# A two-layer RG-LRU / stick-breaking attention trunk: splits moved between engines, an output projection two tiles at a time, the last attention heads in another order

## The chip, the cores and the metric

The kernel runs on one core of a Trainium2 chip. Time is what the device takes for one execution, in microseconds (us), as the median of several runs. The engines are TensorE (PE; its weight loads are listed apart as PEld), VectorE (DVE), ScalarE (ACT), GpSimd (POOL) and SyncE (SP), which issues most of the transfers. Each engine works through a queue of its own in order; between engines semaphores say what has to be done before.

## What is computed

Two layers on x of 512 positions by 1024 features, all float32. Each layer is a token mixer and a dense FFN, each behind an RMS norm and with its result added to x. The first mixer is a gated linear recurrence, the second stick-breaking attention with 16 heads of 64.

```python
def reference(x, ...):
    for layer in range(DEPTH):
        h = _rmsnorm(x, norm_mix_g[layer])
        ...
        x = x + mix          # layer 0: _rglru_mixer, layer 1: _sb_mixer
        h = _rmsnorm(x, norm_ffn_g[layer])
        x = x + _swiglu(h, ffn_w_gate[layer], ffn_w_up[layer], ffn_w_down[layer])
    return _rmsnorm(x, final_g)

def _rglru_mixer(...):
    gate, xc = gelu(gate_br), conv(x_br)
    a, u = ...                        # from two block matrices w_r, w_i
    hs = _linear_scan(a, u)
    return (hs * gate) @ w_out

def _stick_breaking_attention(q, k, v):   # per block of queries
    z = einsum("bhqd,bhkd->bhqk", qb, k32) * scale
    log_1m = where(mask, log_sigmoid(-z), 0.0)
    suffix = cumsum(log_1m, axis=3, reverse=True) - log_1m
    wts = where(mask, exp(log_sigmoid(z) + suffix), 0.0)
    return einsum("bhqk,bhkd->bhqd", wts, v32)

def _swiglu(h, w_gate, w_up, w_down):     # inner width 2816
    return (silu(h @ w_gate) * (h @ w_up)) @ w_down
```

## The kernel before

**Products in three matmuls.** To hold float32 accuracy every operand is split into a rounded high part and the rest, and a product is wh·xh + wh·xl + wl·xh: mm3, L348 to L351 (the FFN has its own at L762 to L764). Weights come in chunks of 128x1024. For each chunk, split_piece makes wh (a copy on ACT, L303) and wl = raw - wh (L304). Which engine does L304 is set by wl_engine: for chunks 0 to 19 by the table wl_on (L191), in the FFN by Piece.pool, and otherwise by the chunk's parity (odd on POOL) unless wl_dve is set.

**The stream of chunks.** chunk() hands the next split chunk to PE's code, and on the way splits ahead (two chunks, or as many as its argument says) and has SP load ahead. There are three buffers for wh and wl each and four for raw chunks, so a split waits until PE is done with an older chunk.

**Stages.** rglru() comes first: the two branches of w_in, the gates, the scan, the product ah/al of scan and gate (L650 to L653), and the recurrent output projection (from L716): eight tiles m, each one bank of eight k-steps over the pairs ah, al, then an add into x[m]. In this stage the scheduler picks the order by priority. Chunk 18 is a weight tile of the gate branch. Then ffn(0), attention(), ffn(1) and the last norm. In the FFN and in the attention loop the written order stands as it is on PE, ACT, DVE and POOL.

**FFN.** The weights are combined in the manner of Strassen's method. A unit u (six to an FFN, the last one smaller) has pieces for the up and gate products and seven down products; DownPiece q makes the weight d_q of one of these. d5 is the one used just ahead of the product whose bank L922 adds into b (called q2 below: its two halves start at L922). L144 is a subtraction of two raw tiles on POOL that makes the operand of a later piece.

**Attention.** After v, the loop over h (L1252) is written in steps. Step h holds: half of a projection for tile t = h+3 (from h = 13 on, where no projection is left, a part of the output projection instead), s1(h+1) (scores, three banks), chain_a(h+1) (ACT L1138 to L1140, DVE L1141 and L1142, POOL L1143), the projection's other half, s3(h-1) (weights times v, L1201), s2(h) (the suffix sums as matmuls, L1175), chain_b(h) (exponentials on ACT, L1188 and L1189; awl on DVE, L1190), and s3_evac(h-1), which forms o for a head (ACT copy L1214, DVE add L1215). osplit(p) splits o of two heads into oh (ACT L1234) and ol (DVE L1235). out_part(m, lo, hi) multiplies k-steps lo to hi-1 of output tile m; out_evac adds the bank into x[m] (L1248).

**Banks.** Of the eight PSUM banks six hold the scores of two heads (three each, alternating). The last two (list mb) serve projections and s3. From h = 13 on one of them, fill, holds output tile 0, so s3(h-1) must wait until s3_evac(h-2) has emptied the other.

Of the kernel before, what the change touches and what calls it, by code (L numbers as in the profile page):

```python
# [132 lines left out]
class DownPiece(Piece):  # L133
    def __init__(self, unit, q):
        self.unit, self.q, self.c = unit, q, 0
        self.pool = q in (5, 7, 4) and not unit.direct
        self.summed = False
# [33 lines left out]
class Kern:  # L171
    def __init__(self, ctx, tc, a, out):
        self.ctx, self.tc, self.nc, self.a, self.out = ctx, tc, tc.nc, a, out
        mk = lambda name, bufs, **kw: ctx.enter_context(tc.tile_pool(name=name, bufs=bufs, **kw))
        self.const = mk("const", 1)
        self.wp = mk("wp", 1)
        self.tp = mk("tp", 1)
        self.ar = mk("ar", 1)
        self.free = deque((0, i) for i in range(NS1))
        self.free2 = deque()  # L180
        self.clock = 0
        self.keep2 = 0
        self.slot = {}
        pp = mk("pp", 1, space=bass.MemoryType.PSUM)
        self.bank = [pp.tile([P, S], F32, name=f"bank{i}") for i in range(8)]
        self.bi = 0
        self.tn = 0
        self.later, self.done, self.chain = [], set(), {}
        self.wl_dve = False
        self.ring4 = None  # L190
        self.wl_on = {**dict.fromkeys((*range(5, 12), 14), self.nc.gpsimd),  # L191
                      **dict.fromkeys((2, 3, 4, 12, 13, 15, 16, 17, 18, 19), self.nc.vector)}
# [109 lines left out]
    def split_piece(self, i, raw, wh, wl, c):  # L302
        self.nc.scalar.copy(wh[:, c], raw[:, c])  # L303
        self.wl_engine(i).tensor_tensor(wl[:, c], raw[:, c], wh[:, c].bitcast(F32), ALU.subtract)  # L304
# [262 lines left out]
    def rglru(self):  # L567
        nc, tc = self.nc, self.tc
        with ExitStack() as cx:
# [147 lines left out]
            self.bi = 0  # L717
            for m in range(KT):
                p = self.ps()
                self.mm_tile(p, ys)  # L720
                nc.vector.tensor_tensor(self.x[m], self.x[m], p, ALU.add)
                self.ffn_in(m, "g_ffn0")
# [290 lines left out]
    def attention(self):  # L1013
# [5 lines left out]
        with ExitStack() as cx:  # L1019
# [198 lines left out]
            with tc.manual_schedule(engines={E.PE, E.Activation, E.DVE, E.Pool}):  # L1218
# [21 lines left out]
                def out_part(m, lo, hi, bank=None):  # L1240
                    if m not in outs:
                        outs[m] = (bank, *self.chunk(1 if m == 2 else None))
                    pt, wh, wl = outs[m]
                    for k in range(lo, hi):
                        self.mm3(pt, wh[:, ts(k)], wl[:, ts(k)], *ou[k], k == 0, k == KT - 1)

                def out_evac(m):
                    nc.vector.tensor_tensor(self.x[m], self.x[m], outs.pop(m)[0], ALU.add)  # L1248
                    self.ffn_in(m, "g_ffn1")

                nsp = 0
                for h in range(NH + 1):  # L1252
# [6 lines left out]
                    elif h == 13:  # L1259
                        fill = mps()  # L1260
                        out_part(0, 0, 3, fill)
                    elif h == 14:
                        out_part(0, 3, 6)
                    elif h == 15:
                        out_part(1, 0, 6, self.bank[0])
                    elif h == 16:
                        out_part(0, 6, 7)
                        out_part(1, 6, 7)
                        out_part(2, 0, 4, self.bank[1])
                    if h + 1 < NH:  # L1270
                        s1(h + 1)
                        chain_a(h + 1, (0, 1))
                    if t < 16 and h != 1:
# [6 lines left out]
                    if h >= 1:  # L1280
# [6 lines left out]
                    if h < NH:  # L1287
                        s2(h)
                        chain_b(h)
                    if h >= 1:  # L1290
# [3 lines left out]
                    if 6 <= h < 14 and 2 * nsp + 1 < h:  # L1294
                        osplit(nsp)
                        nsp += 1
                    if h == 14:
                        osplit(6)
                out_part(2, 4, 7)
                osplit(7)  # L1300
# [92 lines left out]
```

## Time and profile before

| | |
|---|---|
| time, median of 3 runs | 1119.3 us (1119.23 to 1120.44) |
| the profiled execution's own time | 1120.95 us |
| its span in the profile | 1119.3 us |
| mean granted TensorE clock | 0.997 |
| moved by transfers | 159.87 MB, a mean of 143 GB/s |
| costliest groups outside PE | DVE L304, 118 of wl<-raw,wh: 188.1 us; ACT L303, 144 of wh<-raw: 145.3 us |

A row of the time line reads: start, duration, engine, line, operation, out<-in by the program's names, size, count, and in brackets the idle time of the engine just before with what ended it. Several alike rows are joined into one with a count (x2). A matmul's duration reaches to its modelled end, so the distance of two starts, not the duration, says how fast matmuls follow each other. A row of the table of waits reads: engine and line, what it waited for, total us, times, longest.

### The profile page before, as it was taken

The page shows a single profiled execution, that of the slowest core. Times are in us where ns is not written, and L with a number is a line of the kernel's source. Part 1 is how long each engine was busy: PE and PEld are TensorE (multiplying, and loading weights), DVE is VectorE, ACT ScalarE, POOL GpSimd, SP SyncE. Part 2 cuts the span into 40 slices and gives each one's busy share as a digit, 9 for nine tenths or more (in the row PEclk, how much of TensorE's full clock was granted, in tenths as well). Part 3 has the DMA queues.
Part 4 walks back from the last instruction along what each step waited for, and adds up shares of the span by engine and source line. Part 5 has one row for each costly group of instructions (what it writes and reads, how often), then busy time and mean ns, then how long its engine had stood idle before and what let it go on. Part 6 is the DMA issues. An engine that isn't in the chain of part 4 may idle for free.

```text
span 1119.3 us, 14757 instructions
## 1 busy us (share of the span) xinstructions
PE 1095.9 (98%) x5265; PEld 907.9 (81%) x5265; DVE 907.5 (81%) x1250; ACT 711.7 (64%) x1086; POOL 381.9 (34%) x258
## 2 busy tenths in 40 slices
PE   9999999999999999999999999899999999999996
PEld 6887788878888888888888888778887888888885
DVE  7878886697888888987378898868669787888997
ACT  7598567465646464535389998967764555646454
POOL 2352232335151614205043444312233435261411
PEclk9999999999999999999999999999999999999999
DMA  8522328877676766342243423223986767665421
GB/s 282 171 75 81 126 95 203 192 169 206 157 202 156 201 157 182 83 145 95 79 121 98 118 76 94 77 73 123 212 181 169 192 146 213 157 196 119 150 66 75
DMA packets 48825, 159.87 MB, mean 143 GB/s; under 512 B 6000, under 2 KB 7280, under 8 KB 48752
## 3 DMA queue, kind: packets, MB, share of 16 engines
q1 hardware_dynamic: 36368, 113.84, 29.8%
q0 software_dynamic: 12384, 45.09, 23.1%
q8 instruction: 41, 0.67, 0.2%
q14 instruction: 32, 0.26, 0.1%
HBM read 148.43 MB, written 2.10 MB: 134 GB/s over the span
## 4 chain that ended last, share of the span: by engine, by line
PE 68%; DVE 12%; ACT 4%; issue 4%; DMA 3%; POOL 0%; SPq 0%; DVEq 0%; POOLq 0%; ACTq 0%
PE bank L762 14%; PE bank L763 14%; PE bank L764 14%; PE bank L349 6%; PE bank L351 6%; PE bank L350 5%; DVE wl L304 5%; PE bank L1175 3%; DMA bu<-w_gu 2%; ACT wh L303 2%; PE bank L1201 2%; DVE y L754 1%; PE bank L769 1%; PE bank L1120 1%; DMA bv<-w_gu 1%
## 5 line engine op out<-in xcount | busy, mean ns | idle before, releaser
L304 DVE TENSOR_TENSOR wl<-raw,wh 128x1024 fp32r<-128x1024 f32 (+1 forms) x118 | 188.1, 1599 | 44.1 <-ACT wh L303 43.8
L303 ACT CAST wh<-raw 128x1024 fp32r<-128x1024 f32 (+1 forms) x144 | 145.3, 1012 | 94.5 <-PE bank L764 39.1
L762 PE MATMUL bank<-wh,ow 128*128 128x512 f32 (+1 forms) x480 | 180.0, 375 | 3.4 <-DVE u L754 1.7
L763 PE MATMUL bank<-wl,ow 128*128 128x512 f32 (+1 forms) x480 | 178.6, 372 | 0.6 <-DVE wl L304 0.5
L764 PE MATMUL bank<-wh,ow 128*128 128x512 f32 (+1 forms) x480 | 178.3, 372 | 0.0
L92 POOL DMA_DIRECT2D bu<-w_gu x64 | 55.9, 874 | 271.9 <-DVE wl L304 95.4
L303 ACT CAST wh<-bu 128x1024 fp32r<-128x1024 f32 x66 | 69.4, 1052 | 67.5 <-PE bank L764 37.9
L304 DVE TENSOR_TENSOR wl<-bu,wh 128x1024 fp32r<-128x1024 f32 x66 | 82.0, 1260 | 32.4 <-ACT wh L303 31.5
L762 PEld LDWEIGHTS bank<-wh,ow 128*128 128x128 f32 x480 | 90.4, 188 | 21.2 <-issue 3.2
L349 PE MATMUL bank<-uh,wh 128*128 128x512 f32 x256 | 102.7, 401 | 1.3 <-DVE t L1085 0.6
L763 PEld LDWEIGHTS bank<-wl,ow 128*128 128x128 f32 x480 | 90.4, 188 | 16.5 <-DVE wl L304 1.4
L764 PEld LDWEIGHTS bank<-wh,ow 128*128 128x128 f32 x480 | 90.4, 188 | 15.6
L351 PE MATMUL bank<-uh,wl 128*128 128x512 f32 x256 | 100.2, 392 | 1.0 <-DVE wl L304 1.0
L350 PE MATMUL bank<-ul,wh 128*128 128x512 f32 x256 | 99.8, 390 | 0.3 <-DVE ul L406 0.3
L304 POOL TENSOR_TENSOR wl<-raw,wh 128x1024 fp32r<-128x1024 f32 (+1 forms) x26 | 59.2, 2278 | 111.8 <-ACT wh L303 111.8
L754 DVE TENSOR_TENSOR y<-y,bank 128x512 f32<-128x512 f32 x140 | 88.8, 677 | 2.4 <-PE bank L764 2.3
L762 PE MATMUL bank<-wh,hth 128*128 128x512 f32 x192 | 75.2, 392 | 0.0
L764 PE MATMUL bank<-wh,htl 128*128 128x512 f32 x192 | 74.8, 389 | 0.0
L763 PE MATMUL bank<-wl,hth 128*128 128x512 f32 x192 | 74.7, 389 | 0.0
L304 DVE TENSOR_TENSOR wl<-bv,wh 128x1024 fp32r<-128x1024 f32 x44 | 58.3, 1336 | 15.3 <-ACT wh L303 15.2
L1143 POOL TENSOR_TENSOR spl<-t,sph 128x512 fp32r<-128x512 f32 (+1 forms) x32 | 36.3, 1156 | 85.6 <-DVE sph L1142 79.8
L303 ACT CAST wh<-bv 128x1024 fp32r<-128x1024 f32 x44 | 46.1, 1050 | 20.4 <-DMA bv<-w_gu 9.6
(257 smaller groups left out, 2798.8 us busy)
## 6 DMA issues: line engine op xcount, KB each, us to landing
bu<-w_gu POOLq DMA_DIRECT2D x64, 512.0 KB, 5.8
raw<-w_gu SPq DMA_DIRECT2D x44, 512.0 KB, 3.4
raw<-w_dn SPq DMA_DIRECT2D x24, 512.0 KB, 6.0
bu<-w_gu SPq DMA_DIRECT2D x22, 512.0 KB, 4.2
bv<-w_gu SPq DMA_DIRECT2D x22, 512.0 KB, 4.3
bv<-w_gu POOLq DMA_DIRECT2D x22, 512.0 KB, 6.5
d<-w_dn SPq DMA_DIRECT2D x20, 512.0 KB, 4.0
raw<-w_qk SPq DMA_DIRECT2D x16, 512.0 KB, 3.4
```

The lines of the kernel that those rows point to most:

```text
L92: kern.soon(lambda: kern.nc.gpsimd.dma_start(t, self.part(n), accum_op=ALU.add))
L303: self.nc.scalar.copy(wh[:, c], raw[:, c])
L304: self.wl_engine(i).tensor_tensor(wl[:, c], raw[:, c], wh[:, c].bitcast(F32), ALU.subtract)
L349: mm(out, lhsT=wh, rhs=xh, start=first, stop=False)
L350: mm(out, lhsT=wh, rhs=xl, start=False, stop=False)
L351: mm(out, lhsT=wl, rhs=xh, start=False, stop=last)
L754: add = lambda o, a, b: nc.vector.tensor_tensor(o, a, b, ALU.add)
L762: mm(out, lhsT=xh, rhs=wh, start=first, stop=False, skip_group_check=True)
L763: mm(out, lhsT=xh, rhs=wl, start=False, stop=False, skip_group_check=True)
L764: mm(out, lhsT=xl, rhs=wh, start=False, stop=last, skip_group_check=True)
L1143: nc.gpsimd.tensor_tensor(sl[:, w], sp[:, w], sh[:, w].bitcast(F32), ALU.subtract)
L1175: mm(zt[kt][:, o0:o0 + ZW[j]], lhsT=tri if j == kt else one_n, rhs=s_, start=False, stop=True, skip_group_check=True)
```

## The change

Four things, in four places.

- **Table wl_on:** wl of chunk 18 is made on POOL instead of DVE.
- **Recurrent output projection:** tiles 0 and 1 go together, in two banks: k-steps 0 to 4 of both, then 5 and 6 of both, then 7 of both. Their two adds follow together.
- **FFN:** wl of d5 is made on DVE instead of POOL, in the units that have it there (u = 1 to 4, both FFNs).
- **Attention:** osplit(0) to osplit(5) are put off from the end of a step to the next step, behind chain_a's first two banks; osplit(6) from the end of step 14 to the start of step 15; osplit(7) comes ahead of the last out_parts. Output tile 0 is taken in two sums: its k-steps 0 to 5 close the bank fill and are added to x[0] in step 14; k-steps 6 and 7 go to another bank at the end and are added then. fill then takes tile 1, and tile 2 has bank 0 to itself. s3(14) stands behind s2(15) and chain_b(15). The splits of w_bo[1] and w_bo[2] are written out at the end of steps 13 and 15, with wh on DVE instead of ACT; so on DVE wh and wl of w_bo[2] stand behind the three awl of chain_b(15), where before wl alone stood ahead of them. w_bo[1]'s wl stays on POOL.

```diff
--- before.py
+++ after.py
@@ -133,7 +133,7 @@
 class DownPiece(Piece):
     def __init__(self, unit, q):
         self.unit, self.q, self.c = unit, q, 0
-        self.pool = q in (5, 7, 4) and not unit.direct
+        self.pool = q in (7, 4) and not unit.direct
         self.summed = False
 
     def ready(self):
@@ -186,10 +186,10 @@
         self.bi = 0
         self.tn = 0
         self.later, self.done, self.chain = [], set(), {}
-        self.wl_dve = False
+        self.wl_dve = self.wh_dve = False
         self.ring4 = None
-        self.wl_on = {**dict.fromkeys((*range(5, 12), 14), self.nc.gpsimd),
-                      **dict.fromkeys((2, 3, 4, 12, 13, 15, 16, 17, 18, 19), self.nc.vector)}
+        self.wl_on = {**dict.fromkeys((*range(5, 12), 14, 18), self.nc.gpsimd),
+                      **dict.fromkeys((2, 3, 4, 12, 13, 15, 16, 17, 19), self.nc.vector)}
 
     def ps(self):
         b = self.bank[self.bi % 8]
@@ -300,7 +300,10 @@
         return wh, wl
 
     def split_piece(self, i, raw, wh, wl, c):
-        self.nc.scalar.copy(wh[:, c], raw[:, c])
+        if self.wh_dve:
+            self.nc.vector.tensor_copy(wh[:, c], raw[:, c])
+        else:
+            self.nc.scalar.copy(wh[:, c], raw[:, c])
         self.wl_engine(i).tensor_tensor(wl[:, c], raw[:, c], wh[:, c].bitcast(F32), ALU.subtract)
 
     def split_one(self):
@@ -715,9 +718,17 @@
             self.free_u()
             ys = list(zip(ah, al))
             self.bi = 0
+            two = [(self.ps(), *self.chunk()) for _ in range(2)]
+            for lo, hi in ((0, 5), (5, 7), (7, 8)):
+                for p, wh, wl in two:
+                    for k in range(lo, hi):
+                        self.mm3(p, wh[:, ts(k)], wl[:, ts(k)], *ys[k], k == 0, k == KT - 1)
             for m in range(KT):
-                p = self.ps()
-                self.mm_tile(p, ys)
+                if m < 2:
+                    p = two[m][0]
+                else:
+                    p = self.ps()
+                    self.mm_tile(p, ys)
                 nc.vector.tensor_tensor(self.x[m], self.x[m], p, ALU.add)
                 self.ffn_in(m, "g_ffn0")
             for hl in ys:
@@ -1237,18 +1248,30 @@
 
                 outs = {}
 
-                def out_part(m, lo, hi, bank=None):
+                def out_part(m, lo, hi, bank=None, stop=KT):
                     if m not in outs:
-                        outs[m] = (bank, *self.chunk(1 if m == 2 else None))
-                    pt, wh, wl = outs[m]
+                        outs[m] = [None, *self.chunk(1 if m < 3 else None), 0]
+                    e = outs[m]
+                    if bank is not None:
+                        e[0], e[3] = bank, lo
                     for k in range(lo, hi):
-                        self.mm3(pt, wh[:, ts(k)], wl[:, ts(k)], *ou[k], k == 0, k == KT - 1)
+                        self.mm3(e[0], e[1][:, ts(k)], e[2][:, ts(k)], *ou[k], k == e[3], k == stop - 1)
+
+                def out_add(m):
+                    nc.vector.tensor_tensor(self.x[m], self.x[m], outs[m][0], ALU.add)
 
                 def out_evac(m):
-                    nc.vector.tensor_tensor(self.x[m], self.x[m], outs.pop(m)[0], ALU.add)
+                    out_add(m)
+                    outs.pop(m)
                     self.ffn_in(m, "g_ffn1")
 
+                def out_split():
+                    self.wh_dve = True
+                    self.split_one()
+                    self.wh_dve = False
+
                 nsp = 0
+                due = None
                 for h in range(NH + 1):
                     t = h + 3
                     if t < 16:
@@ -1258,18 +1281,22 @@
                             proj_evac1(t)
                     elif h == 13:
                         fill = mps()
-                        out_part(0, 0, 3, fill)
+                        out_part(0, 0, 3, fill, 6)
                     elif h == 14:
-                        out_part(0, 3, 6)
+                        out_part(0, 3, 6, None, 6)
                     elif h == 15:
-                        out_part(1, 0, 6, self.bank[0])
+                        osplit(6)
+                        out_part(1, 0, 6, fill)
                     elif h == 16:
-                        out_part(0, 6, 7)
-                        out_part(1, 6, 7)
-                        out_part(2, 0, 4, self.bank[1])
+                        out_part(2, 0, 4, self.bank[0])
                     if h + 1 < NH:
                         s1(h + 1)
+                        if h == 14:
+                            out_add(0)
                         chain_a(h + 1, (0, 1))
+                    if due is not None:
+                        osplit(due)
+                        due = None
                     if t < 16 and h != 1:
                         proj(t, 1)
                         proj_evac1(t)
@@ -1277,7 +1304,7 @@
                         chain_a(h + 1, (2,))
                     if h >= 13:
                         mb[:] = [b_ for b_ in (self.bank[6], self.bank[7]) if b_ is not fill]
-                    if h >= 1:
+                    if 1 <= h and h != 15:
                         s3(h - 1)
                     if t < 16 and t % 2:
                         proj_evac2(t)
@@ -1287,17 +1314,21 @@
                     if h < NH:
                         s2(h)
                         chain_b(h)
+                    if h == 15:
+                        s3(h - 1)
+                    if h in (13, 15):
+                        out_split()
                     if h >= 1:
                         s3_evac(h - 1)
                     if t < 16 and t % 2 == 0:
                         proj_evac2(t)
                     if 6 <= h < 14 and 2 * nsp + 1 < h:
-                        osplit(nsp)
+                        due = nsp
                         nsp += 1
-                    if h == 14:
-                        osplit(6)
+                osplit(7)
                 out_part(2, 4, 7)
-                osplit(7)
+                out_part(1, 6, 7)
+                out_part(0, 6, 7, self.bank[1])
             for m in range(3):
                 out_part(m, 7, 8)
                 if m == 0:
```

The order of DVE at the end of the recurrent block, from the last gate product but one to the first add into x. al_489, al_529 and al_613 are the low parts for k = 5, 6 and 7, the chunk's wl belongs to w_ao. Before:

```order
L651 TENSOR_TENSOR bank_75<-bank_75,sv_852 128x512
L701 TENSOR_TENSOR bank_76<-bank_76,acc 128x512
L304 TENSOR_TENSOR wl_1137<-raw_1028,wh_1136 128x1024
L653 TENSOR_TENSOR al_489<-bank_74,ah_488 128x512
L653 TENSOR_TENSOR al_529<-bank_75,ah_528 128x512
L651 TENSOR_TENSOR bank_76<-bank_76,sv_871 128x512
L653 TENSOR_TENSOR al_613<-bank_76,ah_612 128x512
L721 TENSOR_TENSOR x_78<-x_78,bank_70 128x512
```

In the changed kernel:

```order
L654 TENSOR_TENSOR bank_75<-bank_75,sv_852 128x512
L656 TENSOR_TENSOR al_489<-bank_74,ah_488 128x512
L656 TENSOR_TENSOR al_529<-bank_75,ah_528 128x512
L704 TENSOR_TENSOR bank_76<-bank_76,acc 128x512
L307 TENSOR_TENSOR wl_1101<-raw_1028,wh_1100 128x1024
L654 TENSOR_TENSOR bank_76<-bank_76,sv_871 128x512
L656 TENSOR_TENSOR al_613<-bank_76,ah_612 128x512
L732 TENSOR_TENSOR x_78<-x_78,bank_70 128x512
L732 TENSOR_TENSOR x_79<-x_79,bank_71 128x512
```

al of k = 5 and 6 now stand ahead of the gate add (L701, now L704) and of the wl; the two adds into x follow each other.

The order of DVE in the FFN, unit 1 of the first FFN, from the wl that follows the sum into b to q2 (L922). d_190 is d5's source, its wl is wl_2090. Before:

```order
L304 TENSOR_TENSOR wl_2069<-raw_1755,wh_2068 128x1024
L754 TENSOR_TENSOR y_1499<-y_1499,bank_76 128x512
L754 TENSOR_TENSOR y_1500<-y_1500,bank_77 128x512
L304 TENSOR_TENSOR wl_2109<-raw_1944,wh_2108 128x1024
L304 TENSOR_TENSOR wl_2129<-raw_1980,wh_2128 128x1024
L922 SCALAR_TENSOR_TENSOR b_1497<-b_1497,nrs,bank_72 128x512
L922 SCALAR_TENSOR_TENSOR b_1498<-b_1498,nrs,bank_73 128x512
```

In the changed kernel (all lines 3 to 11 higher):

```order
L307 TENSOR_TENSOR wl_2069<-raw_1755,wh_2068 128x1024
L765 TENSOR_TENSOR y_1499<-y_1499,bank_76 128x512
L765 TENSOR_TENSOR y_1500<-y_1500,bank_77 128x512
L307 TENSOR_TENSOR wl_2090<-d_190_1751,wh_2089 128x1024
L307 TENSOR_TENSOR wl_2109<-raw_1944,wh_2108 128x1024
L307 TENSOR_TENSOR wl_2129<-raw_1980,wh_2128 128x1024
L933 SCALAR_TENSOR_TENSOR b_1497<-b_1497,nrs,bank_72 128x512
L933 SCALAR_TENSOR_TENSOR b_1498<-b_1498,nrs,bank_73 128x512
```

One wl, d5's, has come in ahead of the two that stand before q2; on POOL the same row is gone.

The order of ACT in step 13 of the attention, from the copy for o(11) (t_6425) to the first exponential of chain_b(13) (awh). oh is osplit(5), wh_6432 a chunk of w_bo, t are chain_a(14)'s. Before:

```order
L1214 COPY t_6425<-bank_76 64x512
L1234 CAST oh_6428<-o_6246 128x512
L303 CAST wh_6432<-raw_6039 128x1024
L1138 ACTIVATE t_6459<-bank_70 128x512
L1139 ACTIVATE t_6459<-t_6459 128x512
L1140 ACTIVATE t_6459<-t_6459 128x512
L1138 ACTIVATE t_6469<-bank_71 128x384
L1139 ACTIVATE t_6469<-t_6469 128x384
L1140 ACTIVATE t_6469<-t_6469 128x384
L1138 ACTIVATE t_6479<-bank_72 128x384
L1139 ACTIVATE t_6479<-t_6479 128x384
L1140 ACTIVATE t_6479<-t_6479 128x384
```

In the changed kernel:

```order
L1225 COPY t_6425<-bank_76 64x512
L1149 ACTIVATE t_6449<-bank_70 128x512
L1150 ACTIVATE t_6449<-t_6449 128x512
L1151 ACTIVATE t_6449<-t_6449 128x512
L1149 ACTIVATE t_6459<-bank_71 128x384
L1150 ACTIVATE t_6459<-t_6459 128x384
L1151 ACTIVATE t_6459<-t_6459 128x384
L1245 CAST oh_6469<-o_6246 128x512
L1149 ACTIVATE t_6473<-bank_72 128x384
L1150 ACTIVATE t_6473<-t_6473 128x384
L1151 ACTIVATE t_6473<-t_6473 128x384
L1199 ACTIVATE awh_6507<-bank_73 128x512
```

The oh copy has moved from ahead of the chain to behind its first two banks, and the chunk's copy is gone from ACT at this place.

## The prediction

> **What bounds the kernel now.** I read the page's first part, then the table of what TensorE (PE) waits for, then the time line of PE at those waits.
>
> ```profile
> span 1119.3 us, 14757 instructions
> PE 1095.9 (98%) x5265; PEld 907.9 (81%) x5265; DVE 907.5 (81%) x1250; ACT 711.7 (64%) x1086; POOL 381.9 (34%) x258
> PE bank L1120 <- DVE awl L1190: 2.9, 3, 2.3
> PE bank L762 <- DVE b L922: 1.7, 3, 1.0
> 698.07 0.39 PE L349 MATMUL bank<-uh,wh 128*128 128x512 f32 x1
> 698.30 0.39 PE L350 MATMUL bank<-ul,wh 128*128 128x512 f32 x1
> ```
>
> PE is busy 98% and sets the end; the change takes no matmul away, so only PE's waits can be won. They are small and scattered (waits rows: total, times, longest). Undisturbed 128x512 matmuls start 0.23 us apart (698.07, 698.30), exactly 0.227 over longer stretches; what two starts are further apart than that I call lost. The change touches three of the places: the recurrent block, the FFN's L922, and attention's last heads. All else on PE I take as it is.
>
> **Recurrent block: wl of chunk 18 to POOL, output projection two tiles at a time.**
>
> ```profile
> 103.56 1.99 ACT L303 CAST wh<-raw 128x1024 fp32r<-128x1024 f32 x2
> 108.95 0.39 PE L350 MATMUL bank<-ul,wh 128*128 128x512 f32 x1
> 109.09 2.33 DVE L304 TENSOR_TENSOR wl<-raw,wh 128x1024 fp32r<-128x1024 f32 x2
> 110.34 0.50 PE L351 MATMUL bank<-uh,wl 128*128 128x512 f32 x1 [1.00 <-DVE wl L304]
> 116.61 2.39 POOL L304 TENSOR_TENSOR wl<-raw,wh 128x1024 fp32r<-128x1024 f32 x1 [20.59 <-ACT wh L303]
> 116.73 3.36 DVE L304 TENSOR_TENSOR wl<-raw,wh 128x1024 fp32r<-128x1024 f32 x1
> 124.59 0.50 PE L349 MATMUL bank<-ah,wh 128*128 128x512 f32 x1
> 125.47 1.28 DVE L653 TENSOR_TENSOR al<-bank,ah 128x512 fp32r<-128x512 f32 x2
> 126.21 0.50 PE L350 MATMUL bank<-al,wh 128*128 128x512 f32 x1 [1.12 <-DVE al L653]
> 128.01 0.69 DVE L653 TENSOR_TENSOR al<-bank,ah 128x512 fp32r<-128x512 f32 x1 [0.65 <-ACT ah L652]
> ```
>
> PE could have run the first matmul on chunk 18's wl at 108.95+0.23=109.18 and ran it at 110.34: 1.16 lost, 0.16 more than the bracket, because a restarted matmul takes longer (0.50 against 0.39); after such a restart the next start is another 0.11 late. wl stood last in a DVE queue. POOL idles 20.59 before 116.61, so it can take wl as soon as its wh is there: the first of the two casts of 103.56 ends near 104.6, and with 2.39 to 3.5 (the free and the held length, next paragraph) wl is done by 107.0 to 108.1, before 109.18. That wait goes: 1.27.
>
> What is late next: while a POOL op with SBUF operands runs, a DVE op whose two inputs lie in SBUF stands still, and the reverse. Row 116.73 shows it: one wl takes 3.36, against 2.33/2=1.17 each at 109.09, beside POOL's 2.39 at 116.61. So DVE may lose up to 2.39 there, wins the 1.17 of the moved wl, and is some 1.2 late. The projection then starts at 120.9-1.27=119.6 (124.59, less its wait of 0.29, less 15 matmuls of 0.227, gives 120.9). Before, it lost at 124.59 (0.29), at 126.21 (126.21-124.59-0.23=1.39, and 0.11 behind), and 0.43 at the last ah: 2.22. With two tiles interleaved, 30 matmuls (6.8 us) stand ahead of the first use of k=5 instead of 15: needed at 119.6+6.8+0.2=126.6 (al of k=5), 127.3 (k=6) and 119.6+42x0.227=129.2, al 129.4 (k=7). DVE delivered these at 126.1, 126.75 (row 125.47) and 128.70 (row 128.01). Delivered at the same times they cost nothing; all 1.2 late they cost about 0.7. But the order shows al of k=5 and 6 moved ahead of a gate add (0.6) and a wl split (1.2), which pays for the 1.2, so I take nothing. Sum 1.27+2.22=3.5; between 1.5 (both lost in part) and 4: **-3.5**.
>
> **FFN: wl of d5 from POOL to DVE, in 8 units (u=1 to 4 of both FFNs).**
>
> ```profile
> 242.78 1.05 ACT L303 CAST wh<-d 128x1024 fp32r<-128x1024 f32 x1
> 245.94 2.73 POOL L304 TENSOR_TENSOR wl<-d,wh 128x1024 fp32r<-128x1024 f32 x1
> 246.60 6.50 DVE L304 TENSOR_TENSOR wl<-raw,wh 128x1024 fp32r<-128x1024 f32 x2 [1.26 <-ACT wh L303]
> 248.75 3.27 POOL L144 TENSOR_TENSOR d<-raw,raw 128x1024 f32<-128x1024 f32 x1
> 253.03 1.39 DVE L922 SCALAR_TENSOR_TENSOR b<-b,nrs,bank 128x512 f32<-128x512 f32 x2
> 253.91 0.47 PE L762 MATMUL bank<-wh,ow 128*128 128x512 f32 x1 [0.32 <-DVE b L922]
> 856.77 7.20 DVE L304 TENSOR_TENSOR wl<-raw,wh 128x1024 fp32r<-128x1024 f32 x2 [1.42 <-ACT wh L303]
> 864.77 0.47 PE L762 MATMUL bank<-wh,ow 128*128 128x512 f32 x1 [1.01 <-DVE b L922]
> 983.20 0.47 PE L762 MATMUL bank<-wh,ow 128*128 128x512 f32 x1 [0.36 <-DVE b L922]
> ```
>
> L922 (named q2 here) is queued on DVE behind two wl, which take 6.50 and 7.20 instead of 2.33: POOL's wl (2.73) and L144 (3.27) hold them. In three units PE waits for q2: 0.32+1.01+0.36, and 0.16 more at each, 2.2 in all. In the new order d5's wl stands on DVE just ahead of those two. Its wh is there at 243.83, and DVE idles 1.26 before 246.60, so its 1.17 fits into idle time. POOL is left with L144, which can hold DVE for 3.27 at most: 2.33+3.27=5.6 at most against 6.50, with d5's wl paid from the idle slot, so q2 comes 0.9 to 2.6 earlier, more than two of the waits and, at 856.77 (7.20), more than the third. L144's result feeds pieces that come later than q2. Value **-2.2**; the upper end is the second rival's.
>
> **Attention, steps 12 to 16.**
>
> ```profile
> 697.30 0.47 PE L349 MATMUL bank<-uh,wh 128*128 128x512 f32 x1 [0.61 <-DVE t L1085]
> 710.61 0.50 PE L1120 MATMUL bank<-qh,ks 128*128 128x512 f32 x1 [0.19 <-DVE awl L1190]
> 711.27 0.28 DVE L1154 CAST r<-t 128x256 fp32r<-128x256 f32 x1
> 713.10 0.62 ACT L1234 CAST oh<-o 128x512 fp32r<-128x512 f32 x1 [1.78 <-DVE o L1215]
> 713.12 0.85 PE L1201 MATMUL bank<-awh,vs 128*128 128x512 f32 x4 [0.17 <-DVE o L1215]
> 713.63 1.04 ACT L303 CAST wh<-raw 128x1024 fp32r<-128x1024 f32 x1
> 718.68 0.39 PE L351 MATMUL bank<-oh,wl 128*128 128x512 f32 x1
> 719.51 0.58 ACT L1188 ACTIVATE awh<-bank 128x512 fp32r<-128x512 f32 x1
> 721.37 0.50 PE L1120 MATMUL bank<-qh,ks 128*128 128x512 f32 x1 [2.30 <-DVE awl L1190]
> 726.75 0.46 PE L1175 MATMUL bank<-sph,tri 128*128 128x512 f32 x1
> 729.94 0.50 PE L349 MATMUL bank<-oh,wh 128*128 128x512 f32 x1 [0.68 <-DVE awl L1190]
> 734.03 1.23 DVE L304 TENSOR_TENSOR wl<-raw,wh 128x1024 fp32r<-128x1024 f32 x1 [0.26 <-ACT wh L303]
> 723.40:726.80 3.40, 3.40 (x15) 3.11 (x15) 2.60 (x6) 3.25 (x7) 0.68 (x1) 0.54 0.01 2
> ```
>
> Lost now: at 697.30, 0.8; around 710.61 and 713.12, 1.5 with the bank waits inside s1; from 718.91 (the end of 718.68's pitch) to 726.75, 7.84 go for an s1 and an s3 that take 1.63 and 1.22 where nothing disturbs them, so 5.0, of which 1.6 is the granted clock of 0.54 (last row: time, then busy us of PE, PEld, DVE, ACT, POOL, then the clock); at 729.94, 0.95. Together 8.25.
>
> The cause is ACT's order: at the end of step 12 ACT waits 1.78 for o, does oh, then copies wh for 1.04, and only then starts the chain of the next head; so chain_b(13) reaches 719.51, DVE's awl follows, and s1(15) waits 2.30. In the new order osplit stands behind the first two chains and the wh copy of w_bo[1] is on DVE. ACT's chain_b(13) comes earlier by 1.78+1.04 and by about 1.1 gained ahead of it: 715.6. Worked through the new order, PE waits: at 697.30 none; step 13 0.8; step 14: s1(15) needs three banks, and their awl come at 717.4, 718.7 and 719.4 (715.6 with the same 1.8 behind it as from 719.51 to 721.3, and two more); PE is there at 717.4 (718.91 less the 1.5 won before), 718.0 and 719.1, so it waits 0.75 and 0.25, then 1.0 for s3(13), because DVE does the wh copy (0.6) and o(12) (0.7) behind that last awl, to 721.0, where PE is ready at 720.05; step 15 none; step 16 2.3, because w_bo[2]'s wh and wl now both stand on DVE behind awl(15) (near 733.4): wh +0.6, wl +1.23, so 734.0 and 735.2, where PE is ready near 732.4. Sum 5.1, so 8.25-5.1: **-3.1**.
>
> A wh copy of 128x1024 on DVE has no row. A CAST of 128x256 takes 0.28 (711.27), so four times its elements at most 1.1; a two-input op of 128x1024 takes 1.23; the same cast starts its next op 0.20 later, so it may be as short as 0.5. I take 0.6; at 1.2 each of the two copies costs 0.6 more. The two k=6 parts at the end and the second x[0] add (one 0.7 DVE op under matmuls) cost nothing as long as PE has out_part(2) to run.
>
> **Behind the recurrent block.** The first FFN starts under a chain of transfers.
>
> ```profile
> 170.92 5.80 DMA bu<-w_gu
> 213.95 5.52 DMA bu<-w_gu
> ```
>
> Between 222 and 232 PE waits some 2 us for what these bring. The first is issued by POOL behind an op that follows PE's sums, so it should move with PE; where it doesn't, up to 3.5 is given back. I take **+0.5**.
>
> Sum: -3.5-2.2-3.1+0.5=-8.3. The profiled execution took 1120.95 for a span of 1119.3; by -8.3 it becomes 1112.65, a span of 1111.0. The median of the runs is 1119.3, 1.65 below the profiled execution's own time, so the forecast for the median is **1111.0**.
>
> **Rivals.**
> 1. The recurrent gain is swallowed by the transfers of the first FFN. For it: PE waits there although it stands far behind in the queue. Against it: the issue hangs on PE's own progress. +3: 1114.
> 2. Slower: d5's wl makes DVE later. If POOL's ops (L144, then the next wl) still hold both wl, the added 1.2 and up to 0.7 of a longer hold (3.27 against 2.73) put q2 1.2 to 1.9 late in all 8 units. The three without slack pay in full, the others in part (no PE wait there now): at 1.9 some 3x1.9+5x1.0=11 over before's level in place of -2.2, so 1119.3-6.1+11=1124. It turns the sign from about 1.2 per unit (3x1.2+5x0.5=6.1). Against it: DVE's idle slot of 1.26 and one POOL op fewer. The Trainium skill (page "SBUF — State Buffer", section "Who interferes with whom") says that a VectorE instruction with two SBUF inputs and a GpSimd one that reads SBUF exclude each other, the first to issue holding the port to its end; that speaks against moving work to DVE wherever POOL still runs, and the 6.50 of row 246.60 agrees. By the rule with L144 first, it is the loss of the gain, 1113; by L144 behind d5's wl, 1111.
> 3. The new waits of step 14 (2.0 within 4 us) or step 16 (2.3) bring the clock down again, as the 2.30 at 721.37 did: 1.6 each, or the copy is 1.2. 1113 to 1114.5. The Trainium skill (page "TensorE: Matmul & The Clock Gate", section "HAM oscillation — how this bites in real kernels") sets the danger at idle gaps above about 3.4 us; by that none of these waits would throttle and the sum stays. The trace differs: clock 0.54 behind a wait of 2.30, so I keep the rival.
> 4. The change doesn't do what it says: the scheduler in the recurrent block already fills PE's waits with the next tile's matmuls, and the new waits of steps 14 and 16 eat the attention term: 1116.
>
> **Numbers.** Forecast 1111 (within 1.5): 0.52; clock or copy: 0.18; transfers: 0.14; the fourth, or two together (1116): 0.07; d5 slower: 0.05; better, with steps 13 to 16 free of waits (1106): 0.04. The range 1107.5 to 1116.5 leaves out 1124, 1106 and some of the rest, less than 0.2. A measurement of this kernel tells apart about 0.2% (2.2 us): faster means under 1117.1. That is all but 2 and part of 4: 0.89; within 0.06; slower 0.05.
>
> **What would show it.** Right: PE has no wait for wl near 109 and none for al near 126; the row "PE bank L762 <- DVE b" is gone, and the two wl ahead of q2 take about 5; no clock under 0.9 near 723; PE waits about 2 us for w_bo[2]'s wl near the end of attention. Wrong, if wl of d5 takes over 3 us on DVE; if PE's wait between 222 and 232 grows by what was won at 110 and 126; if the granted clock drops in step 14 or 16; if the wh copy on DVE takes over 1.

## The result, and the profile after

The changed kernel takes 1113.25 us in the median (1110.91 to 1116.54, 6 runs), the kernel before 1120.22 in the runs beside it (1119.23 to 1121.40, 6 runs): a ratio of 0.994, 95% interval 0.9924 to 0.9957. That is 7.0 us less; forecast were 8.3 less and 1111.0. The profiled execution took 1113.21 for a span of 1111.5, 7.8 less than the span before.

The first rows are the engines' busy time and the waits of PE in the changed kernel (engine, line, what it waited for: total us, times, longest). Line 762 of before is 773 now, 349 is 352, 350 is 353, 351 is 354, 1120 is 1131.

```profile
PE 1092.8 (98%) x5265; PEld 908.7 (82%) x5265; DVE 901.6 (81%) x1260; ACT 710.0 (64%) x1084; POOL 359.9 (32%) x251
PE bank L354 <- DVE wl L307: 2.0, 3, 1.1
PE bank L352 <- DVE wh L304: 1.4, 1, 1.4
PE bank L1212 <- DVE o L1226: 0.8, 2, 0.7
PE bank L1131 <- DVE awl L1201: 0.4, 1, 0.4
```

The rows of L762 for L922 and of L350 for al are gone, and s1's waits for awl have gone from 2.9 to 0.4. New are a wait for wh made by DVE and, in place of the one for wl at 110, two at 121 and 731 (the third lies in the first 10 us). The next rows, from time lines of PE and DVE in the changed kernel, place them: the recurrent block, the two wl ahead of q2, and attention's step 16.

```profile
121.30 0.50 PE L354 MATMUL bank<-ah,wl 128*128 128x512 f32 x1 [1.07 <-DVE wl L307]
241.41 1.22 DVE L307 TENSOR_TENSOR wl<-d,wh 128x1024 fp32r<-128x1024 f32 x1
242.80 4.52 DVE L307 TENSOR_TENSOR wl<-raw,wh 128x1024 fp32r<-128x1024 f32 x2 [0.17 <-ACT wh L306]
717.00 0.85 PE L1212 MATMUL bank<-awh,vs 128*128 128x512 f32 x4 [0.65 <-DVE o L1226]
729.96 0.50 PE L352 MATMUL bank<-oh,wh 128*128 128x512 f32 x1 [1.44 <-DVE wh L304]
731.22 0.51 PE L354 MATMUL bank<-oh,wl 128*128 128x512 f32 x1 [0.53 <-DVE wl L307]
```

To see where the 7.8 come from, take the start of one and the same matmul in both profiles (each has 5265) at the borders of five stretches. The table gives the change of each stretch against the kernel before, for every profile of this study; times in the head are those of the kernel before, and "rest" is the start of the span, where the clock starts up at another moment each time (-0.4 to 2.8 up to 104 us), and up to 0.4 between 330 and 680.

| profile | 104 to 132: recurrent block | 215 to 247: start of the first FFN | 247 to 330 and 840 to 990: units with d5 | 680 to 752: attention's end | rest | span |
|---|---|---|---|---|---|---|
| before (us) | 27.8 | 31.9 | 233.1 | 72.1 | | 1119.3 |
| changed | -2.2 | -1.6 | -2.5 | -1.8 | +0.3 | 1111.5 |
| changed, again | -2.3 | -2.0 | -2.4 | -3.4 | +1.0 | 1110.3 |
| recurrent part alone | -2.2 | -2.2 | -0.1 | -0.5 | +0.6 | 1114.9 |
| wl of chunk 18 alone | +3.0 | -0.9 | -1.2 | +1.1 | +0.3 | 1121.6 |
| two tiles alone | -2.2 | -2.1 | +0.7 | +1.2 | +3.1 | 1119.8 |
| d5 alone | 0.0 | -0.2 | -2.1 | -0.1 | -0.2 | 1116.7 |
| attention alone | 0.0 | -0.8 | 0.0 | -3.3 | 0.0 | 1115.2 |
| changed, d7 too | -2.2 | -0.7 | -1.9 | -1.8 | +0.7 | 1113.4 |
| changed, wh copies on ACT | -2.3 | -2.0 | -2.5 | -2.5 | +1.3 | 1111.4 |
| changed, osplit at the end of its step | -2.2 | -2.3 | -2.5 | +0.9 | +0.3 | 1113.5 |
| changed, w_bo[2] split early | -2.2 | -0.4 | -2.5 | -5.8 | +1.8 | 1110.3 |
| three mends | -3.6 | -2.4 | -1.4 | -6.4 | +0.3 | 1105.8 |

A stretch that a kernel leaves as it was still differs from the kernel before: the units with d5 by -1.2 to +0.7, attention's end by -0.5 to +1.2 (there the clock was low for one cell of 3.41 us or for two). A single entry of about 1 therefore shows nothing by itself; the waits behind it have to say the same.

### The profile page after: what moved, and what is told of

The parts are those of the page before. It is cut to its first block, busy times and chain, and to the rows that moved or that the text cites. A ratio compares the mean times of both kernels' runs of the same rounds, so it can differ in the third digit from the quotient of the medians.

```text
span 1111.5 us, 14758 instructions
## 1 busy us (share of the span) xinstructions
PE 1092.8 (98%) x5265; PEld 908.7 (82%) x5265; DVE 901.6 (81%) x1260; ACT 710.0 (64%) x1084; POOL 359.9 (32%) x251
## 4 chain that ended last, share of the span: by engine, by line
PE 76%; DVE 9%; ACT 3%; issue 2%; DMA 1%; POOL 0%; DVEq 0%; ACTq 0%; POOLq 0%
PE bank L773 16%; PE bank L774 16%; PE bank L775 16%; PE bank L352 7%; PE bank L354 7%; PE bank L353 7%; DVE wl L307 4%; PE bank L1186 3%; PE bank L1212 2%; DVE y L765 1%; PE bank L780 1%; DMA bu<-w_gu 1%; PE bank L1131 1%; ACT wh L306 1%; PE bank L1132 1%
## 5 line engine op out<-in xcount | busy, mean ns | idle before, releaser
L307 DVE TENSOR_TENSOR wl<-raw,wh 128x1024 fp32r<-128x1024 f32 (+1 forms) x117 | 176.4, 1511 | 37.6 <-ACT wh L306 37.4
L307 POOL TENSOR_TENSOR wl<-raw,wh 128x1024 fp32r<-128x1024 f32 (+1 forms) x27 | 62.1, 2301 | 101.9 <-ACT wh L306 99.4
L765 DVE TENSOR_TENSOR y<-y,bank 128x512 f32<-128x512 f32 x140 | 88.9, 679 | 2.4 <-PE bank L775 2.3
L1154 POOL TENSOR_TENSOR spl<-t,sph 128x512 fp32r<-128x512 f32 (+1 forms) x32 | 39.1, 1244 | 84.1 <-DVE sph L1153 81.2
```

Source lines behind the costliest of these rows:

```text
L765: add = lambda o, a, b: nc.vector.tensor_tensor(o, a, b, ALU.add)
L1154: nc.gpsimd.tensor_tensor(sl[:, w], sp[:, w], sh[:, w].bitcast(F32), ALU.subtract)
```

## The experiments

**The parts alone.** Three kernels take the kernel before and add one part each.

Recurrent part:

```diff
-        (5..11, 14) POOL; (..., 16, 17, 18, 19) DVE
+        (5..11, 14, 18) POOL; (..., 16, 17, 19) DVE
+            two = [(self.ps(), *self.chunk()) for _ in range(2)]
...
```

> The kernel before with the recurrent block's part alone (wl of chunk 18 on POOL, two tiles at a time). Theory (the parts add up, each where the profile after shows it): the wait of 1.00 at 110.34 goes, those at 124 to 128 go, one of about 1.1 comes on the first wl of w_ao, so 2.1 us are won up to 130; and the 2.1 lost between 222 and 232 falls to about 0.6, since the transfers move with PE. Span 1119.3-3.6=1115.7, ratio about 0.997. Rival (the gain near 222 came from another part, or by chance): the loss between 222 and 232 stays at 2.1 or grows, span 1117.2 or more, ratio 0.998 to 1.0.

Measured: 1117.28, ratio 0.9975 (0.9963 to 0.9987), span 1114.9. The waits in the block are those seen in the changed kernel, to 0.1 us: -2.2. The stretch from 215 on gains 2.2 too; whether that belongs to the change is taken up below.

d5:

```diff
-        self.pool = q in (5, 7, 4) and not unit.direct
+        self.pool = q in (7, 4) and not unit.direct
```

> The kernel before with d5's wl on DVE alone. Theory: the three waits for L922 go (2.2 us), the two wl ahead of it take 4 to 5 us instead of 6.5; span 1117.1, ratio 0.998. Rival (DVE only gets later, and the waits went because the units start at another time in the changed kernel): the waits stay or grow, ratio 1.0 or more.

Measured: 1118.5, ratio 0.9988 (0.9975 to 1.0000), span 1116.7. The interval reaches 1, so the times alone don't show the gain; the trace does. The row of L762 for L922 is gone from PE's waits. One new wait of 0.92 for another DVE op (L754, at 241.82) stands ahead of d5's place, behind a transfer that took 6.79 (226.16 to 232.95); the units from 247 on gain 2.1.

Attention (all that the change does from out_part on, and no more):

```diff
-                        osplit(nsp)
+                        due = nsp
...
+                    if h in (13, 15):
+                        out_split()
```

> The kernel before with the attention part alone. Theory: the waits from step 12 to 14 fall from 8.2 to about 2.8, and step 16 brings a wait of 1.4 and one of 0.5 for w_bo[2]'s split on DVE, with the clock near 0.5 for some 3.4 us behind them (1.6 us); net -1.5 to -2, span 1117.5, ratio 0.998. Rival (the half-speed stretch behind step 16 is an accident of one execution): no clock under 0.9 there, net -3.3, span 1116, ratio 0.997.

Measured: 1117.15, ratio 0.9973 (0.9961 to 0.9984), span 1115.2, attention -3.3. Both waits of step 16 are there (1.44 and 0.53) but the clock stays up behind them, so the rival was right. The granted clock is the last figure but two of each row: first the changed kernel's profile, then this one, each with the waits in the first two rows.

```profile
728.40:731.80 3.40, 1.43 (x7) 0.79 (x5) 3.09 (x5) 0.90 (x2) 0.00 (x0) 1.00 0.02 5
731.80:735.20 3.40, 3.40 (x10) 2.62 (x8) 0.00 (x0) 0.00 (x0) 0.00 (x0) 0.50 0.43 154
```

```profile
729.80:733.20 3.40, 2.80 (x21) 2.56 (x19) 1.81 (x4) 3.05 (x7) 0.00 (x0) 1.00 0.00 0
733.20:736.60 3.40, 2.03 (x8) 1.38 (x9) 2.60 (x4) 0.20 (x1) 0.00 (x0) 1.00 0.11 17
```

The clock's records change on a grid of 3.41 us. In the changed kernel both waits fell into one cell of it (of the 7 matmuls in the row 4 begin there, the others are left over from the cell before), and the next cell ran at 0.50. Here the border at 733.2 cuts the first wait (732.60 to 734.04), and the second lies in the next cell.

By their ratios the three parts save 0.25, 0.12 and 0.27%, 0.64% together, and the whole change 0.60%: they add up within the intervals. The spans of the single profiles add up to more (11.1 against 7.8), because the start of the first FFN (3.2 in the three together, 1.6 in the whole) and attention's end with its clock (3.9 and 1.8) come out otherwise in each execution.

**The recurrent block taken apart.** One kernel only moves the wl of chunk 18, the other only takes the two tiles together.

```diff
-        (5..11, 14) POOL; (..., 16, 17, 18, 19) DVE
+        (5..11, 14, 18) POOL; (..., 16, 17, 19) DVE
```

> The kernel before with wl of chunk 18 on POOL and nothing else. Theory (POOL's op wins the wait at 110 and holds two of DVE's two-input ops up by 2.2, so that what follows on DVE is late): the 1.27 at 110 goes; the first wl of w_ao comes late and costs about 1.3 there, and the waits for al near 124 to 128 stay at 2.2 or are hidden by it in part; 104 to 131.5 gains 0 to 1.3 in all. Rival (the wait on w_ao's wl comes from the two-tile order): no such wait, 1.3 won.

Measured: one run, 1123.31 (before 1119.20 to 1123.42 beside it); the block is 3.0 longer, so theory and rival both missed. The wait at 110 goes (-1.3), but at the other end the kernel loses more than before:

```profile
105.53 3.42 DVE L642 TENSOR_TENSOR xc<-xc,sv 128x512 f32<-128x512 f32 x2
118.22 2.84 DVE L304 TENSOR_TENSOR wl<-raw,wh 128x1024 fp32r<-128x1024 f32 x1
121.11 0.50 PE L351 MATMUL bank<-ah,wl 128*128 128x512 f32 x1 [1.03 <-DVE wl L304]
128.56 0.51 PE L349 MATMUL bank<-ah,wh 128*128 128x512 f32 x1 [2.12 <-ACT ah L652]
130.50:133.90 3.40, 3.40 (x9) 2.68 (x9) 2.57 (x3) 2.07 (x5) 2.38 (x1) 0.50 0.01 2
```

Two adds of xc take 3.42 where 1.27 is usual (row 105.66 of before), held by POOL's wl, which runs from 104.55 to 107.80. DVE is 2.2 late behind them and still some 1 late once the wl that it no longer makes is taken off. The first wl of w_ao ends at 121.06 in place of 120.09, and PE waits 1.03 for it and 2.12 for the last ah, with no second tile to cover it. The low clock behind these waits is about 1.6 of the loss (an estimate: 8 of the 9 matmuls in the last row begin in that cell, where 15 fit at 0.227).

```diff
-                p = self.ps()
-                self.mm_tile(p, ys)
+            two = [(self.ps(), *self.chunk()) for _ in range(2)]
...
```

> The kernel before with the first two tiles of the recurrent output projection together, wl of chunk 18 still on DVE. Theory: the wait of 1.00 at 110.34 stays, w_ao's first wl comes in time, the three waits at 124 to 128 go: 2.2 won between 118 and 131.5. Rival: the wait on w_ao's wl is there too, 0.9 won.

Measured: one run, 1121.5 (1119.8 span, with a start-up 2.8 longer than before's). The block gains 2.2 with the wait at 110 still there and no wait for w_ao's wl. So the two tiles alone bring what the whole part brings: the move of wl to POOL wins 1.3 at 110 and gives 1.3 back at 121. The theory was right.

**d7 to DVE too.**

```diff
-        self.pool = q in (7, 4) and not unit.direct
+        self.pool = q == 4 and not unit.direct
```

> The changed kernel with d7's wl on DVE too (POOL then keeps d4's alone). It asks how far the FFN's gain carries. Theory (d5 won because DVE had an idle slot of 1.26 at its place and POOL's op held two of DVE's): at d7's place the sequence on DVE gets 1.2 longer; where it has an idle slot nothing is lost, so within 1 us of the changed kernel, ratio to before 0.993 to 0.995. Rival (each op moved to DVE wins, since POOL holds DVE up for longer than the op costs it): 1 to 3 us faster, 0.991 to 0.993. The second rival of the prediction, at this place: new waits of PE for DVE in 8 units, 3 us or more slower, 0.997 or more.

Measured: 1112.79, ratio 0.9921 (0.9902 to 0.9940). No wait for L933 (q2) comes; the units with d5 are 0.6 slower than in the changed kernel, most of it one wait (0.31) for L765 ahead of d5's place. The ratio lies in the range of the first rival (0.991 to 0.993), but its interval overlaps that of the changed kernel, and the trace shows nothing won at d7's place, as the theory had it. The slower rival is out at this place too.

**Attention's last steps.** First w_bo[2] is split at the start of step 15, where ACT idles 1.53 (row 724.59 of the changed kernel) ahead of oh.

```diff
                         osplit(6)
+                        self.split_one()      # ahead of osplit(6)
...
-                    if h in (13, 15):
+                    if h == 13:
```

> The changed kernel, with w_bo[2] split at the start of step 15 instead of its end: wh on ACT, in its idle 1.5 us ahead of oh, wl on DVE ahead of ol. Theory (the split's late place makes the wait in step 16, and the wait makes the low clock): both waits of step 16 go (1.6+0.7 with their restarts) and the clock stays at 1.0 (1.6 and 0.2 more), so 4.1 us under the changed kernel: span 1107.4, ratio to before 0.989. Rival (DVE is the limit there wherever the split stands): awl of step 15 come 1.2 later and the wait only moves to s3(15) or stays for awl, span 1109.5 to 1111.5, ratio 0.991 to 0.994.

Measured: 1110.37, ratio 0.9906 (0.9892 to 0.9921), span 1110.3 with a start 1.6 later than the changed kernel's. Attention's end gains 4.0 over the first profile of the changed kernel and 2.4 over the second; both waits are gone, and none takes their place.

Then two kernels put back one half of the new order each: the wh copies on ACT again, and osplit(0) to osplit(5) at the end of their steps.

```diff
-                    self.wh_dve = True      # in out_split: wh on ACT again
...
-                        due = nsp           # the other kernel
+                        osplit(nsp)
```

> The changed kernel with the wh copies of w_bo[1] and w_bo[2] back on ACT, at the same places (end of steps 13 and 15). Theory (it is the order on ACT that won; a copy of 1.05 there puts the next head's chain 1.05 later, which the 0.60 on DVE doesn't): s3(13) starts up to 0.3 earlier, but chain_a(15) and with it what s2(15) needs 1.05 later; w_bo[2]'s wl ends about 0.4 later on the path awl(15), wh, wl. Steps 12 to 16 lose 0.5 to 1.5 against the changed kernel, the low clock aside. Rival (the engine of the copies doesn't matter): the same within 0.2.

Measured: one run, 1113.09. Attention's end is at -2.5, with low clock behind step 16:

```profile
717.30 0.85 PE L1212 MATMUL bank<-awh,vs 128*128 128x512 f32 x4 [0.34 <-DVE o L1226]
730.48 0.75 PE L352 MATMUL bank<-oh,wh 128*128 128x512 f32 x1 [1.64 <-ACT wh L306]
```

The profile of the changed kernel that has the low clock too is at -1.8, so this one is 0.7 better, where the theory had it 0.5 to 1.5 worse and the rival the same within 0.2. s3(13) waits 0.34 in place of 0.65, as the theory said; but the late chain_a(15) is covered, and for w_bo[2] PE waits 1.64 once in place of 1.44 and 0.53. One profile each: that the copies on DVE cost 0.7 is not shown, but they won nothing here.

> The changed kernel with osplit(0) to osplit(5) back at the end of their steps; the rest as changed. Theory (ACT's idle wait for o ahead of oh, 1.78 at the end of step 12, was the larger half): the 0.8 at 697 comes back and chain_b(13) is about 2.4 late, so that s1(15) waits some 2.5 to 3 in place of 1.0; steps 11 to 14 lose 2.5 to 3.5 against the changed kernel. Rival (the wh copies were the cause): under 1 lost.

Measured: one run, 1115.18. Attention's end is at +0.9, 2.7 worse than the first profile of the changed kernel and 4.3 worse than the second. The waits of before are back, though s1(15) waits 1.33 and not 2.30 as before, nor the 2.5 to 3 of the theory:

```profile
692.46 0.47 PE L352 MATMUL bank<-uh,wh 128*128 128x512 f32 x1 [0.59 <-DVE t L1096]
715.58 0.50 PE L1131 MATMUL bank<-qh,ks 128*128 128x512 f32 x1 [1.33 <-DVE awl L1201]
719.20:722.60 3.40, 3.40 (x12) 3.00 (x12) 3.08 (x7) 2.57 (x6) 3.39 (x3) 0.50 0.21 57
```

So the deferred osplit is the part that won; the clock falls here behind step 14, and stays up behind step 16. That s1(15) waits 1.0 less than before fits the copy of 1.04 that ACT no longer makes (not tested by itself).

**The changed kernel again.**

> The changed kernel once more, for what differs between executions. Theory: the waits at 121, 714, 717 and the two of step 16 are the same within 0.1; the stretch from 215 to 235 differs by up to 1.5 from the first profile, since the same stretch differs as much among kernels that are alike up to there; the clock falls behind step 16 only if both waits lie in one stretch of the clock's grid. Rival: 215 to 235 repeats within 0.2, and the low clock comes each time.

Measured: one run, 1111.98. The waits at 121, 714 and 717 repeat within 0.1, and this time the clock stays up, with the same two waits of step 16:

```profile
727.00:730.40 3.40, 1.96 (x16) 1.72 (x14) 2.43 (x5) 2.73 (x7) 0.00 (x0) 1.00 0.00 0
730.40:733.80 3.40, 2.88 (x11) 2.09 (x12) 1.79 (x2) 0.00 (x0) 0.00 (x0) 1.00 0.34 92
```

215 to 247 differs by 0.4 from the first profile, less than the theory allowed.

**Three mends together:** w_bo[2] split early, w_bo[1]'s split behind o(12) instead of ahead of it, and the wl of w_ao's first tile on POOL, of its second on DVE.

```diff
-        (5..11, 14, 18) POOL; (..., 16, 17, 19) DVE
+        (5..11, 14, 18, 20) POOL; (..., 16, 17, 19, 21) DVE
...
+                        self.split_one()      # step 15, ahead of osplit(6)
...
                         s3_evac(h - 1)
+                    if h == 13:
+                        out_split()
```

> The changed kernel with three mends: w_bo[2] split at the start of step 15 as in the run before; w_bo[1]'s split behind o(12) instead of ahead of it; and the wl of the first two w_ao tiles exchanged (the first on POOL, the second on DVE). Theory: 4.1 in step 16 with the low clock, 0.6 of the 0.85 that s3(13) waits for o(12), and the 1.35 for w_ao's first wl: 6 under the changed kernel, span 1105.5 when the first FFN starts as in the profile of the changed kernel; ratio to before 0.9875. Rival (the wait for w_ao's wl only moves to al, which has 0.3 to 1 us to spare): 1.3 less won, ratio 0.989.

Measured: 1108.32 (1107.38 to 1109.21), ratio 0.988 (0.9861 to 0.9900), span 1105.8: the fastest kernel of the study, 0.6% under the changed one by the two ratios, whose intervals don't meet. The recurrent block comes to -3.6, so the rival is out. The whole kernel's longest waits for DVE, the start-up aside, are now among these:

```profile
PE bank L773 <- DVE u L765: 1.8, 2, 0.9
PE bank L773 <- DVE b L765: 0.7, 1, 0.7
PE bank L1131 <- DVE awl L1201: 0.4, 1, 0.4
PE bank L1212 <- DVE o L1226: 0.2, 1, 0.2
```

## Why the prediction was right, point by point

- **What bounds, and the sign.** PE's busy share is 98% still. Of the 7.8, 4.7 are idle time of PE and 3.1 busy time, in which restarts after a wait count; no matmul went. Right.
- **Recurrent block, -3.5 forecast, -2.2 measured.** The waits at 110 and at 124 to 128 went as said. The term was mis-sized in "what is late next". That DVE comes some 1.2 late was about right: two adds lose 2.2 beside POOL (3.44), the wl that DVE no longer makes brings 1.2 back, and gt starts 1.08 later than before (112.42 against 111.34). But I put its cost at al only. The first to suffer was w_ao's first wl, which ended at 120.09 before and ends at 121.25 now, while PE comes for it 1.3 earlier; beside a wl of POOL it ran in both kernels (3.36 before, 2.85 now). PE waits 1.07 for it, 1.3 with the restart. In the kernel before:

```profile
111.34 0.68 DVE L701 TENSOR_TENSOR gt<-bank,acc 128x512 f32<-128x512 f32 x1
```

In the changed kernel:

```profile
105.70 3.44 DVE L645 TENSOR_TENSOR xc<-xc,sv 128x512 f32<-128x512 f32 x2
104.71 3.27 POOL L307 TENSOR_TENSOR wl<-raw,wh 128x1024 fp32r<-128x1024 f32 x1 [8.66 <-ACT wh L306]
112.42 0.68 DVE L704 TENSOR_TENSOR gt<-bank,acc 128x512 f32<-128x512 f32 x1
118.40 2.85 DVE L307 TENSOR_TENSOR wl<-raw,wh 128x1024 fp32r<-128x1024 f32 x1
117.76 2.41 POOL L307 TENSOR_TENSOR wl<-raw,wh 128x1024 fp32r<-128x1024 f32 x1 [9.78 <-ACT wh L306]
```

  With w_ao's first wl on POOL and its second on DVE, in the last kernel, the full 3.6 came.
- **d5, -2.2 forecast, -2.5 measured, -2.1 alone.** The idle slot took d5's wl (241.41), the two wl behind it take 4.52 in place of 6.50, held by POOL's L144 alone (2.39 from 242.72), and no profile with d5 on DVE has a wait for q2. The rival of a later DVE fell. What I took for fixed was not: without the change PE lost 0.9 to 2.2 there, as the profiles of kernels with the old d5 show (the third wait, at 983, was absent in three of four). So the waits that the move ends are worth that much, by the execution, and the forecast had the largest.
- **Attention, -3.1 forecast, -1.8 and -3.4 measured in two profiles of the same kernel, -3.3 alone.** The waits came where the sum had them: 0.6 and 0.85 lost in step 14 (forecast 1.0 and 1.0), 1.6 and 0.7 in step 16 (forecast 2.3). The copy of 128x1024 on DVE, which had no row, lets the next op start 0.60 later (715.67 to 716.27 below), as taken. Of the two causes that the prediction gave together, ACT's wait for o ahead of oh (1.78) and its wh copy (1.04), only the first is borne out: with osplit back at the end of its step the gain goes, with the copies back on ACT it stays. The difference of 1.6 between the two profiles is rival 3: the clock fell behind step 16 in one and not in the other. It was priced right (1.6). With the same two waits it came where both lay in one cell of the clock's grid and not where they lay in two.

```profile
715.67 0.68 DVE L304 CAST wh<-raw 128x1024 fp32r<-128x1024 f32 x1
716.27 0.67 DVE L1226 TENSOR_TENSOR o<-bank,t 64x512 f32<-64x512 f32 x1
```

- **Start of the first FFN, +0.5 forecast, -1.6 measured.** This step was wrong in sign: it feared that the transfers would not move with PE. Without the two tiles together the stretch came to 0 (before), -0.2, -0.8 and -0.9; with them it was -0.4 to -2.4. The transfers there vary from run to run. From the chain of waits of the kernel before and of attention alone (start, duration, transfer):

```profile
185.55 8.90 DMA bv<-w_gu
```

```profile
185.72 6.92 DMA bv<-w_gu
```

  This transfer, of the same code everywhere, took 6.7 to 7.4 in all twelve other profiles, so the one profile that the forecast was made from had a long one at this place. Yet that is not all: PE has no wait left in the stretch in six of the nine profiles with the two tiles together, and in none of the four without them. This speaks for a part that belongs to the two tiles, but the two groups overlap (-0.4 and -0.7 against -0.9), and it stays open how large it is.
- **The sum.** -2.2-1.6-2.5-1.8+0.3=-7.8, against -8.3. It came close partly by luck, because misses cancel: 1.3 less in the block and 1.3 less in attention, against 2.1 more at the FFN's start and 0.3 at d5. In the median the gain is 7.0, and the kernel before came out at 1120.22 beside it, 0.9 above the 1119.3 that the forecast took off from. So the median of 1113.25 lies outside the 1111 within 1.5 that had the largest chance (0.52), and in the 1113 to 1114.5 of the third rival.
- **The signs and the rivals.** All signs of being right are there: no wait for wl near 109 nor for al near 126, the row for L922 gone, 4.52 for the two wl, full clock near 723, 1.44 and 0.53 of waiting for w_bo[2]. One sign of being wrong came too, the low clock behind step 16, in one of two profiles. The first rival (the gain swallowed at the first FFN) and the fourth (the scheduler had filled the waits already, attention wins nothing) are out: the recurrent part alone keeps its 2.2 and gains at the FFN's start, and attention alone is at -3.3.

## What to carry to other kernels

When an op is moved to an idle engine, look at what else it holds up while it runs, and follow the delay to the first consumer, not only to the ones the change was made for: here 1.3 won at one end of a block was lost at the other, and in the kernel with a second exchange it was kept. A split that waits for its input at the end of a step belongs behind the next step's first chain, if the engine works in order; that alone was worth 2.7 to 4.3 us here. And a term read from one execution's transfers or clock is a draw, not a price: two profiles of one kernel differed by 1.6 through the clock alone.

## Not expected of the hardware

The granted clock fell to 0.50 for one or two cells of 3.41 us after full-speed cells in which matmuls filled 0.20 to 0.43 of the time (counted as 0.227 us for each 512 columns of the matmuls that begin in the cell: 0.27 before and in the changed kernel, 0.40 with osplit at the end, 0.43 with the copies on ACT), and never after one with 0.47 (the changed kernel again), 0.53 (attention alone) or more, the first 20 us of the span and its last 12 aside. One such matmul is 0.07 of a cell, so these 13 profiles don't place the border closer than that. PE was never idle for more than 2.30 us at a stretch in these. The Trainium skill (page "TensorE: Matmul & The Clock Gate", section "HAM oscillation — how this bites in real kernels") sets the danger at idle gaps of more than about 3.4 us; here waits of 1.44 and 0.53 in one cell were enough. What the Trainium skill says in the section "What's actually happening" of that page, that the window is free-running, agrees: the same waits cost 1.6 us or nothing, by where the grid fell.
